# Expert weights as consecutive rows per partition, and a float32r scatter, in a two-layer transformer kernel

## The chip, the cores and the metric

The kernel runs on one core of a Trainium2 chip. The metric is the device time of one execution in microseconds (us); the time of a kernel is the median of several runs. Engines: PE is TensorE (matmul; PEld is its weight load), DVE is VectorE, ACT is ScalarE, POOL is GpSimd, and SP is the queue from which the DMAs here are issued. A product has a stationary operand, which is loaded into the array, and a moving operand, which streams through it; its result goes to one of eight PSUM banks.

## What is computed

Two transformer layers on 512 tokens of width 1024, all in float32. The change lies in the last part of the second layer: a mixture of experts in which each expert picks its tokens.

```python
def expert_choice_moe(h, w_router, w_gate, w_up, w_down):
    B, S, D = h.shape                                   # 1, 512, 1024
    cap = max(1, CAPACITY_FACTOR * S // N_EXPERTS)      # 64 tokens for each of 16 experts
    logits = jnp.einsum('bsd,de->bse', h, w_router).astype(jnp.float32)
    aff = jax.nn.softmax(logits, axis=-1)
    gate, idx = lax.top_k(aff.transpose(0, 2, 1), cap)
    xin = jax.vmap(lambda hb, ib: hb[ib])(h, idx)
    hid = jax.nn.silu(jnp.einsum('becd,edf->becf', xin, w_gate)) * jnp.einsum('becd,edf->becf', xin, w_up)
    y = jnp.einsum('becf,efd->becd', hid, w_down) * gate[..., None].astype(h.dtype)
    bidx = jnp.arange(B)[:, None, None]
    return jnp.zeros_like(h).at[bidx, idx].add(y)
```

h is the residual after an RMS norm with a gain, and the result is added to the residual. Each of the 16 experts has three matrices of 1024 x 1024, 4 MB each, so 201 MB in all are read from HBM.

## The kernel before

The program is recorded and not issued at once. A list scheduler with estimated lengths of the instructions puts all of them in an order for each engine, the longest remaining path first, and then issues them; each engine works through its own list strictly. Every instruction is issued in `emit`, so in the trace all carry the line L500, and they are told apart by engine, operation and shape.

The experts are worked through in eight **pairs**; the two experts of a pair use the lower and the upper 64 columns of the array side by side. The residual is `x2`, token-major: 128 tokens on the partitions, four token blocks `tb`, 1024 columns.

- `moe_begin` lists the weights in the order of their use, `ring` gives them eight slots of 2 MB, `load` and `load_to` issue the DMAs on SP as slots come free. A slot holds a half of a matrix: all 1024 rows and 512 columns, with row `128 k + p` on partition p. `pieces` cuts a half into DMAs of mostly 1 MB, four row blocks k each; a run in HBM is 512 columns, 2 KB. The last two halves come as column quarters, so that little work follows the last bytes.
- `ranks(p)` finds for each token its place among those that a pair's two experts could take. PE spreads each affinity over a row (128 x 128 products), VectorE compares (the arrays `ahead`) and counts, PE adds up the counts (128 x 1 products in bfloat16), VectorE puts the place together (`pos`).
- `gather(p)` makes two matrices of 512 tokens x 128 places. `O` has the norm's factor r2 of a token at its place, else zero, and `Og` has the token's affinity, its gate. PE gathers the pair's tokens by products whose stationary operand is 128 neighbouring columns of `x2` and whose moving operand is `O`; the result, already transposed, is scaled by the norm's gain into `XT`. `Og` is transposed into `OGT`.
- `prod(x)` multiplies gathered tokens with the next half of a matrix for both experts: 8 row blocks k, each a float32 product for either expert, 64 places x 512 columns.
- The loop at the end of `moe` makes, for each half h of the hidden columns, gate and up products, `s` = silu(g) * u, and transposes `s` by 128-column blocks into `HT`. Then for each half of the output columns it makes `y`, copies it to `ys`, and scatters: for each token block one float32 product of `OGT` with `ys`, added by VectorE to `acc`. The next pair's `gather` is called between up products and transposes.

## Time and profile before

| | |
|---|---|
| median of 3 runs (lowest to highest) | 3010.46 us (3009.56 to 3010.53) |
| span of the profiled execution, first to last instruction | 3006.1 us |
| PE busy in the span | 2937.9 us, 98% |
| VectorE busy | 1689.4 us, 56% |
| ScalarE busy | 655.6 us, 22% |
| expert loop in the span | 2502.6 to 3006.1, 503.5 us |

The span is the profiled execution's own time; around it lies what the device does before the first and after the last instruction. Busy shares average over stages that are unlike. In the first 2500 us the DMA engines moved around 100 GB/s, in the expert loop 363, so that loop is read on its own below. A group's busy time counts overlapping instructions once; float32 products show as two records each.

### The profile page before, as it was taken

To read this page: it belongs to the slowest core of one execution; us is meant where nothing else is said; L and a number is where in the kernel's file an instruction comes from. 1 tells how busy PE (TensorE), PEld (TensorE's weight loads), DVE (VectorE), ACT (ScalarE), POOL (GpSimd) and SP (SyncE) were. 2 spreads that over 40 slices of the span, in tenths; PEclk is the share of its full clock that TensorE was granted. 3 is DMA by queue.
4 is the path that set the end of the run, shared out by engine and by line. 5 is a ranking of instruction groups with operands and counts; after the bars stand their busy time and mean duration, and the time that the engine had idled before them with its cause. 6 is when DMAs were issued, how large, how long until landed. Compare 5 with 4: busy or idle time off the path is not lost.

```text
span 3006.1 us, 40850 instructions
## 1 busy us (share of the span) xinstructions
PE 2937.9 (98%) x16433; PEld 2274.2 (76%) x16433; DVE 1689.4 (56%) x3270; ACT 655.6 (22%) x1429; POOL 268.9 (9%) x275
## 2 busy tenths in 40 slices
PE   8999999999999999999999999999989999999999
PEld 7888898777888888888987778888778995444443
DVE  6555566776555555555668765555786763223221
ACT  3000124562000110001336620011232541000000
POOL 1000012111000000001121110000231210000000
PEclk9999999999999999999999999999999999999999
DMA  4333322102333333334221033333212367999997
GB/s 122 99 98 98 107 77 56 46 5 82 97 99 95 101 94 96 96 100 113 72 55 39 7 93 98 99 98 98 64 57 86 127 231 259 381 386 386 386 386 282
DMA packets 341091, 403.84 MB, mean 134 GB/s; under 512 B 37209, under 2 KB 242054, under 8 KB 340902
## 3 DMA queue, kind: packets, MB, share of 16 engines
q1 hardware_dynamic: 340742, 401.09, 41.0%
q8 instruction: 129, 2.11, 0.3%
q14 instruction: 60, 0.49, 0.1%
q0 software_dynamic: 160, 0.14, 0.0%
HBM read 399.09 MB, written 2.10 MB: 133 GB/s over the span
## 4 chain that ended last, share of the span: by engine, by line
PE 90%; DVE 6%; ACT 1%; issue 1%; DMA 1%; POOL 0%; SPq 0%; DVEq 0%; ACTq 0%
PE bank L500 90%; DVE arena L500 6%; ACT arena L500 1%; DMA arena<-in_mla_w_ukv 0%; DMA arena<-in_ffn_wg 0%; DMA arena<-in_ffn_wd 0%; POOL arena L500 0%; SPq L500 0%; DVEq L500 0%; ACTq L500 0%
## 5 line engine op out<-in xcount | busy, mean ns | idle before, releaser
L500 PE MATMUL bank<-arena 128*128 128x512 f32 (+9 forms) x16433 | 2937.9, 365 | 64.5 <-DVE arena L500 39.9
L500 PEld LDWEIGHTS bank<-arena 128*128 128x128 f32 (+3 forms) x16065 | 2261.3, 177 | 687.3 <-issue 274.4
L500 DVE TENSOR_TENSOR arena<-arena 128x1024 fp32r<-128x1024 f32 (+10 forms) x906 | 701.5, 791 | 38.7 <-PE bank L500 11.3
L500 DVE CAST arena<-arena 128x1024 fp32r<-128x1024 f32 (+5 forms) x392 | 252.4, 645 | 594.6 <-PE bank L500 423.3
L500 ACT ACTIVATE arena<-arena 128x512 f32<-128x512 f32 (+8 forms) x339 | 199.2, 614 | 857.6 <-DVE arena L500 787.2
L500 POOL TENSOR_TENSOR arena<-arena 128x512 f32<-128x512 f32 (+12 forms) x155 | 193.9, 1260 | 1847.0 <-ACT arena L500 796.3
L500 DVE TENSOR_TENSOR arena<-arena,bank 128x512 f32<-128x512 f32 (+2 forms) x265 | 160.4, 626 | 328.5 <-PE bank L500 327.7
L500 ACT COPY arena<-bank 128x512 f32<-128x512 f32 (+5 forms) x222 | 120.6, 552 | 532.5 <-PE bank L500 529.2
L500 ACT ACTIVATE arena<-bank,arena 128x256 f32<-128x256 f32 (+4 forms) x336 | 162.7, 509 | 236.8 <-DVE arena L500 128.0
L500 ACT CAST arena<-arena 128x512 fp32r<-128x512 f32 (+5 forms) x96 | 77.8, 816 | 503.1 <-DVE arena L500 423.9
L500 DVE TENSOR_TENSOR arena<-bank,arena 128x512 f32<-128x512 f32 (+3 forms) x207 | 134.7, 676 | 67.6 <-PE bank L500 49.2
L500 DVE TENSOR_REDUCE arena<-bank 128x1 f32<-128x512 f32 (+3 forms) x208 | 97.5, 481 | 22.4 <-PE bank L500 20.6
L500 DVE TENSOR_SCALAR arena<-bank,arena 128x128 f32<-128x128 f32 (+4 forms) x100 | 35.6, 395 | 126.2 <-PE bank L500 126.0
L500 DVE TENSOR_SCALAR arena<-arena 128x512 f32<-128x512 f32 (+12 forms) x305 | 95.0, 344 | 12.7 <-ACT arena L500 8.0
L500 DVE SCALAR_TENSOR_TENSOR arena<-arena 128x512 fp32r<-128x512 f32 (+8 forms) x162 | 88.2, 551 | 8.1 <-DMA arena<-in_attn_k_norm_w 4.2
L500 POOL TENSOR_SCALAR arena<-arena 128x512 f32<-128x512 f32 (+3 forms) x93 | 64.8, 698 | 239.9 <-DVE arena L500 207.1
L500 ACT CAST arena<-bank 96x512 fp32r<-96x512 f32 (+3 forms) x97 | 54.3, 580 | 70.2 <-PE bank L500 61.2
L500 PEld LDWEIGHTS <-arena 128*128 128x128 bf16 x368 | 27.4, 97 | 40.5 <-issue 17.9
L500 DVE SCALAR_TENSOR_TENSOR arena<-bank,arena 128x128 bf16<-128x128 f32 (+4 forms) x94 | 40.0, 449 | 31.5 <-PE bank L500 28.8
L500 DVE COPY arena<-bank 128x512 f32<-128x512 f32 (+9 forms) x63 | 34.3, 545 | 34.1 <-PE bank L500 33.1
L500 ACT ACTIVATION_READ_ACCUMULATOR arena<-bank,arena 128x1 f32 x208 | 42.5, 204 | 0.0
L500 ACT ACTIVATE arena<-bank 128x512 f32<-128x512 f32 (+2 forms) x28 | 16.5, 590 | 105.7 <-PE bank L500 86.0
(28 smaller groups left out, 201.3 us busy)
## 6 DMA issues: line engine op xcount, KB each, us to landing
arena<-in_w_expert_gate SPq DMA_DIRECT2D x56, 1024.0 KB
arena<-in_w_expert_up SPq DMA_DIRECT2D x56, 1024.0 KB
arena<-in_w_expert_down SPq DMA_DIRECT2D x48, 1024.0 KB
arena<-in_ffn_wg SPq DMA_DIRECT2D x88, 512.0 KB
arena<-in_ffn_wu SPq DMA_DIRECT2D x88, 512.0 KB
arena<-in_ffn_wd SPq DMA_DIRECT2D x80, 512.0 KB
arena<-in_w_in SPq DMA_DIRECT2D x68, 256.0 KB
arena<-in_w_in SPq DMA_DIRECT2D x32, 512.0 KB
```

What stands on the lines that cost most here:

```text
L500: last[i] = getattr(getattr(self.real, eng), m)(*a, **k).ins
```

## The change

A slot of the ring now holds a half of a matrix by **rows**: partition p has rows 8p to 8p + 3 or 8p + 4 to 8p + 7, all 1024 columns. A DMA of 1 MB takes two neighbouring rows for each partition, a run of 8 KB. The last two loads come in column pieces of 512, 256 and 256.

The contraction then runs over row `8 p + k` on partition p, so the other operands are taken with a step of eight: `x2[:, tb, k::8]` in the gather, `s[:, k::8]` in the transposes, and the gain in that layout, `g8`, by a small DMA of its own.

`prod` works on both column halves at once (two PSUM banks of the tag "a", of which there are four for three), one row half after the other. `s` is whole, 1024 wide, and the next pair's `gather` is called after all up products.

`O` is one exact one-hot matrix, made by one comparison. The norm's factor and the gate are gathered with it: four products of `O` with `fac` (two gates and two copies of r2 per pair) give `GR`, the gate and the factor of each place. The factor enters in silu's scale and in the up product, the gate in `y`. `Og` is gone.

The scatter uses the transposed one-hot `OT` in float32r and splits gated `y` in a rounded part `yh` and the rest `yl`: two float32r products for each token block, added up in PSUM, in place of one float32 product.

```diff
     def moe_begin(self, es):
-        wg, wu, wd = (self.a[f"w_expert_{n}_2"][0] for n in ("gate", "up", "down"))
         self.order = []
         for p in range(self.NE // 2):
-            for h in range(2):
-                for w in (wg, wu):
-                    self.order += [(2 * p + e, w, h) for e in range(2)]
-            for h in range(2):
-                self.order += [(2 * p + e, wd, h) for e in range(2)]
+            for n in ("gate", "up", "down"):
+                w = self.a[f"w_expert_{n}_2"][0]
+                self.order += [(2 * p + e, w, h) for h in range(2) for e in range(2)]
...
-            self.slots.append(p.tile([128, KC, 512], F32, name="ring"))
+            self.slots.append(p.tile([128, KC // 2, D], F32, name="ring"))
...
     def load_to(self, loads):
-        for c, k, m in self.pieces(loads[0][1]) if loads else ():
+        for k, m, c0, c1 in self.pieces(loads[0][1]) if loads else ():
             for t, n in loads:
                 e, w, h = self.order[n]
-                src = w[e].rearrange("(k p) c -> p k c", p=128)[:, k:k + m, 512 * h:512 * h + 512]
                 if n > 70:
                     self.nc.fifo.append(len(self.nc.ops))
-                if c is None:
-                    self.nc.sync.dma_start(t[:, k:k + m], src)
+                if c1 - c0 == D:
+                    src = w[e].rearrange("(p k) c -> p (k c)", k=KC)[:, (4 * h + k) * D:(4 * h + k + m) * D]
+                    self.nc.sync.dma_start(t.rearrange("p k c -> p (k c)")[:, k * D:(k + m) * D], src)
                 else:
-                    self.nc.sync.dma_start(self.split(t)[:, c, k:k + m], src[:, :, 256 * c:256 * c + 256])
+                    src = w[e].rearrange("(p k) c -> p k c", k=KC)[:, 4 * h + k:4 * h + k + m, c0:c1]
+                    self.nc.sync.dma_start(t[:, k:k + m, c0:c1], src)
+    LAST = ((0, 512), (512, 768), (768, 1024))
     def pieces(self, n):
-        m = 4 if 12 <= n < len(self.order) - 4 else 2
         if n < len(self.order) - 2:
-            return [(None, k, m) for k in range(0, KC, m)]
-        return [(c, k, 4) for c in range(2) for k in (0, 4)]
-    def split(self, t):
-        return t.rearrange("p k c -> p (k c)").rearrange("p (h k c) -> p h k c", h=2, k=KC)
+            return [(k, 2, 0, D) for k in (0, 2)]
+        return [(0, 4, c0, c1) for c0, c1 in self.LAST]
...
+        self.g8 = rp.tile([128, KC], F32, name="g8")
+        nc.sync.dma_start(self.g8, self.a["norm2_w_2"][0].rearrange("(p k) -> p k", k=KC))
...
+        fac = rp.tile([128, 4, NE // 2, 4], F32, name="fac")
         nc.vector.tensor_mul(aff, aff, bc(m4))
+        nc.vector.tensor_copy(fac[:, :, :, :2], aff.rearrange("p t (a b) -> p t a b", b=2))
+        nc.vector.tensor_copy(fac[:, :, :, 2:], r2[:, :, None, None].to_broadcast([128, 4, NE // 2, 2]))
...
-            cs = pp.tile([128, 2, 4], F32, name="a", bufs=3)
+            cs = pp.tile([128, 2, 4], F32, name="b", bufs=4)
...
-        XT, OGT = {}, {}
-        g2 = self.gain["norm2_w_2", 0]
+        XT, OT, GR = {}, {}, {}
         def gather(p):
-            O, Og = (mp.tile([128, 4, 2, CAP], F32, name=n, bufs=1) for n in ("O", "Og"))
-            es_ = slice(2 * p, 2 * p + 2)
+            O = mp.tile([128, 4, 2, CAP], F32, name="O", bufs=1)
             pos = ranks(p).rearrange("p e t -> p t e")
-            for tb in range(4):
-                for e in range(2):
-                    nc.vector.tensor_scalar(O[:, tb, e], self.iota, pos[:, tb, e:e + 1], r2[:, tb:tb + 1],
-                                            op0=ALU.is_equal, op1=ALU.mult)
-            nc.vector.tensor_tensor(Og, self.iota[:, None, None, :].to_broadcast([128, 4, 2, CAP]),
+            nc.vector.tensor_tensor(O, self.iota[:, None, None, :].to_broadcast([128, 4, 2, CAP]),
                                     pos[:, :, :, None].to_broadcast([128, 4, 2, CAP]), ALU.is_equal)
-            self.tt("tensor_mul", Og, Og, aff[:, :, es_, None].to_broadcast([128, 4, 2, CAP]))
+            O = [O[:, tb].rearrange("p a b -> p (a b)") for tb in range(4)]
             XT[p] = xp.tile([128, KC, 2 * CAP], F32, name="XT", bufs=2)
             for k0 in range(0, KC, 4):
                 ps = pp.tile([128, 4, 128], F32, name="b", tag="b", bufs=4)
                 for tb in range(4):
                     for d in range(4):
-                        nc.tensor.matmul(ps[:, d, :], x2[:, tb, 128 * (k0 + d):128 * (k0 + d) + 128],
-                                         O[:, tb].rearrange("p a b -> p (a b)"), start=tb + d == 0, stop=tb == 3,
+                        nc.tensor.matmul(ps[:, d, :], x2[:, tb, k0 + d::KC], O[tb], start=tb + d == 0, stop=tb == 3,
                                          skip_group_check=True)
                 for d in range(4):
-                    self.scaled(XT[p][:, k0 + d, :], ps[:, d, :], g2[:, k0 + d:k0 + d + 1])
+                    self.scaled(XT[p][:, k0 + d, :], ps[:, d, :], self.g8[:, k0 + d:k0 + d + 1])
+            ps = pp.tile([128, 4], F32, name="b", bufs=4)
+            for tb in range(4):
+                nc.tensor.matmul(ps, O[tb], fac[:, tb, p], start=tb == 0, stop=tb == 3)
+            GR[p] = mp.tile([128, 2], F32, name="gr", bufs=2)
+            for e in range(2):
+                rows = slice(64 * e, 64 * e + 64)
+                nc.vector.tensor_copy(GR[p][rows], ps[rows, e:3:2 - e])
             ps = pp.tile([128, T], F32, name="b", bufs=4)
             for tb in range(4):
-                nc.tensor.transpose(ps[:, 128 * tb:128 * tb + 128], Og[:, tb].rearrange("p a b -> p (a b)"), self.ident)
-            OGT[p] = mp.tile([128, T], F32, name="OGT", bufs=2)
-            self.copy(OGT[p], ps)
+                nc.tensor.transpose(ps[:, 128 * tb:128 * tb + 128], O[tb], self.ident)
+            OT[p] = mp.tile([128, T], F32R, name="OT", bufs=2)
+            self.copy(OT[p], ps)
         it = [0]
-        def prod(x, c=None):
-            n = 512 if c is None else 256
-            ps = pp.tile([128, n], F32, name="a", bufs=3)
-            ws = [self.slot(it[0] + e) for e in range(2)]
...
-            if c != 0:
+        def prod(x, cols=((0, 512), (512, 1024))):
+            ps = [pp.tile([128, c1 - c0], F32, name="a", tag="a", bufs=4) for c0, c1 in cols]
+            for h in range(2):
+                ws = [self.slot(it[0] + e) for e in range(2)]
+                split = [[c] for c in range(len(cols))] if h and len(cols) > 2 else [range(len(cols))]
+                for cs in split:
+                    for k in range(4):
+                        for c in cs:
+                            with nc.atomic():
+                                for e in range(2):
+                                    nc.tensor.matmul(ps[c][64 * e:64 * e + 64], x[:, 4 * h + k, 64 * e:64 * e + 64],
+                                                     ws[e][:, k, cols[c][0]:cols[c][1]], start=h + k == 0,
+                                                     stop=h == 1 and k == 3, skip_group_check=True)
                 it[0] += 2
                 if it[0] != 4:
                     self.load(2)
...
         outv = self.out
         last = self.NE // 2 - 1
         for p in range(last + 1):
+            gate, r = GR[p][:, 0:1], GR[p][:, 1:2]
+            g = prod(XT[p])
+            if p == 0:
+                e_early.close()
+                ap, hp = pool("moe_acc"), pool("moe_h", "right")
+                acc = ap.tile([128, 4, D], F32, name="acc")
+            s = hp.tile([128, D], F32, name="hs")
+            for c in range(2):
+                nc.scalar.activation(s[:, 512 * c:512 * c + 512], g[c], AF.Silu, scale=r)
+            u = prod(XT[p])
+            for c in range(2):
+                x = s[:, 512 * c:512 * c + 512]
+                nc.vector.scalar_tensor_tensor(x, u[c], r, x, op0=ALU.mult, op1=ALU.mult)
+            if p < last:
+                gather(p + 1)
+            HT = hp.tile([128, KC, 2 * CAP], F32, name="HT")
             for h in range(2):
-                g = prod(XT[p])
-                s = mp.tile([128, 512], F32, name="hs")
-                nc.scalar.activation(s, g, AF.Silu)
-                u = prod(XT[p])
-                nc.vector.tensor_mul(s, s, u)
...
-                if h == 1 and p < last:
-                    gather(p + 1)
                 ps = pp.tile([128, 4, 128], F32, name="b", tag="b", bufs=4)
-                for f in range(4):
-                    nc.tensor.transpose(ps[:, f, :], s[:, 128 * f:128 * f + 128], self.ident)
+                for k in range(4):
+                    nc.tensor.transpose(ps[:, k, :], s[:, 4 * h + k::KC], self.ident)
                 self.copy(HT[:, 4 * h:4 * h + 4, :], ps)
-            for h in range(2):
-                for c in (None,) if p < last or h == 0 else (0, 1):
-                    y = prod(HT, c)
-                    n = 512 if c is None else 256
-                    ys = hp.tile([128, 512], F32, name="ys", bufs=2)[:, :n]
-                    self.copy(ys, y)
-                    for tb in range(4):
-                        ps = pp.tile([128, n], F32, name="b", bufs=4)
-                        nc.tensor.matmul(ps, OGT[p][:, 128 * tb:128 * tb + 128], ys, start=True, stop=True)
-                        at = slice(512 * h + 256 * (c or 0), 512 * h + 256 * (c or 0) + n)
-                        nc.vector.tensor_add(acc[:, tb, at], acc[:, tb, at] if p else x2[:, tb, at], ps)
-                        if p == last:
-                            nc.sync.dma_start(outv[128 * tb:128 * tb + 128, at], acc[:, tb, at])
+            cols = self.LAST if p == last else ((0, 512), (512, 1024))
+            for y, (c0, c1) in zip(prod(HT, cols), cols):
+                n = c1 - c0
+                yh, yl = (hp.tile([128, 512], F32R, name=m, bufs=2)[:, :n] for m in ("yh", "yl"))
+                self.scaled(yh, y, gate)
+                nc.vector.scalar_tensor_tensor(yl, y, gate, f32(yh), op0=ALU.mult, op1=ALU.subtract)
+                for tb in range(4):
+                    ps = pp.tile([128, n], F32, name="b", bufs=4)
+                    o = OT[p][:, 128 * tb:128 * tb + 128]
+                    nc.tensor.matmul(ps, o, yh, start=True, stop=False)
+                    nc.tensor.matmul(ps, o, yl, start=False, stop=True)
+                    nc.vector.tensor_add(acc[:, tb, c0:c1], acc[:, tb, c0:c1] if p else x2[:, tb, c0:c1], ps)
+                    if p == last:
+                        nc.sync.dma_start(outv[128 * tb:128 * tb + 128, c0:c1], acc[:, tb, c0:c1])
```

How the instructions stand on the engines, at the seam between the second and the third pair (the second of seven). On PE, where the scatter ends and the ranks begin; 128x512 rows are the scatter, 128x128 rows the spreading of affinities, 128x1 rows the counts, 64x512 rows expert products. Before:

```order
L500 MATMUL bank_62<-arena 128x512
L500 MATMUL bank_61<-arena 128x512
L500 MATMUL bank_63<-arena 128x128
L500 MATMUL bank_59<-arena 128x128 x4
L500 MATMUL bank_63<-arena 128x128 x3
L500 MATMUL bank_61<-arena 128x128 x4
L500 LDWEIGHTS arena
L500 MATMUL bank_62<-arena 128x1
L500 LDWEIGHTS arena
L500 MATMUL bank_62<-arena 128x1
L500 MATMUL bank_63<-arena 64x512 x2
```

and in the changed kernel:

```order
L500 MATMUL bank_63<-arena 128x512
L500 MATMUL bank_59<-arena 128x512 x2
L500 MATMUL bank_62<-arena 128x512 x2
L500 MATMUL bank_65<-arena 128x512 x2
L500 MATMUL bank_64<-arena 128x128 x4
L500 MATMUL bank_63<-arena 128x128 x4
L500 LDWEIGHTS arena
L500 MATMUL bank_62<-arena 128x1
L500 LDWEIGHTS arena
```

The scatter has two products for each bank, and no expert products stand between the counts.

On PE at the same seam, from the last count over the gather (the 32 products of 128x128) and the transposes of the one-hot matrix and of s, to the next expert products. Before:

```order
L500 MATMUL bank_62<-arena 128x1
L500 MATMUL bank_65<-arena 64x512 x4
L500 MATMUL bank_62<-arena 128x128 x9
L500 MATMUL bank_65<-arena 64x512 x4
L500 MATMUL bank_62<-arena 128x128 x7
L500 MATMUL bank_61<-arena 128x128 x8
L500 MATMUL bank_62<-arena 64x512 x8
L500 MATMUL bank_61<-arena 128x128 x8
L500 MATMUL bank_59<-arena 128x128
L500 MATMUL bank_64<-arena 128x128 x4
```

and in the changed kernel:

```order
L500 MATMUL bank_62<-arena 128x1
L500 MATMUL bank_62<-arena 128x128 x16
L500 MATMUL bank_65<-arena 128x128 x16
L500 MATMUL bank_62<-arena 128x4 x4
L500 MATMUL bank_63<-arena 128x128
L500 MATMUL bank_64<-arena 128x128 x4
L500 MATMUL bank_62<-arena 128x128 x4
L500 MATMUL bank_63<-arena 128x128 x3
L500 MATMUL bank_64<-arena 64x512 x2
```

The gather is one run, with the four GR products (128x4) after it; the expert products that stood around and inside it stand behind the transposes.

On VectorE at the same seam, from the end of the ranks: the place of each token, the matrices for gather and scatter, and what comes next. Before:

```order
L500 TENSOR_REDUCE arena<-arena 128x8
L500 TENSOR_TENSOR arena<-arena 128x8
L500 TENSOR_TENSOR arena<-arena,bank_65 128x8
L500 TENSOR_SCALAR arena<-arena 128x64 x8
L500 TENSOR_SCALAR arena<-bank_65,arena 128x128 x3
L500 TENSOR_SCALAR arena<-bank_61,arena 128x128 x4
L500 TENSOR_TENSOR arena<-arena 128x512 x2
```

and in the changed kernel:

```order
L500 TENSOR_TENSOR arena<-arena,bank_65 128x512
L500 TENSOR_REDUCE arena<-arena 128x8
L500 TENSOR_TENSOR arena<-arena 128x8
L500 TENSOR_TENSOR arena<-arena,bank_62 128x8
L500 TENSOR_TENSOR arena<-arena 128x512
L500 TENSOR_SCALAR arena<-bank_62,arena 128x128 x3
L500 TENSOR_SCALAR arena<-bank_65,arena 128x128 x3
L500 COPY arena<-bank_62 64x2 x2
```

One comparison makes O in place of eight, the product with the gates is gone, and one scatter addition still stands ahead of the place.

## Rows read from the trace of the kernel before

**Rows 1.** expert stage, five stretches: busy us (instructions) by engine, clock, DMA share, GB/s

```profile
2502.60:3006.10 503.50, 492.81 (x2517) 210.67 (x2516) 128.35 (x421) 36.47 (x68) 0.00 (x0) 1.00 0.99 363
2622.50:2683.60 61.10, 61.10 (x324) 27.44 (x322) 17.05 (x58) 4.29 (x8) 0.00 (x0) 1.00 1.05 386
2745.70:2809.20 63.50, 63.15 (x324) 26.95 (x322) 16.36 (x55) 5.75 (x12) 0.00 (x0) 1.00 1.05 386
2809.20:2878.70 69.50, 68.44 (x330) 27.53 (x326) 19.46 (x61) 4.98 (x9) 0.00 (x0) 1.00 1.05 387
2878.70:2943.50 64.80, 62.85 (x321) 26.50 (x320) 17.32 (x58) 4.39 (x8) 0.00 (x0) 1.00 1.04 386
2943.50:3006.10 62.60, 56.59 (x265) 21.27 (x264) 10.93 (x19) 3.69 (x7) 0.00 (x0) 1.00 0.74 261
```

**Rows 2.** PE timeline in the stage: start, us, first instruction, count [idle before]

```profile
2561.24 180.64 PE L500 MATMUL bank<-arena 128*64 128x512 f32 x944 [0.35 <-ACT arena L500]
2742.23 59.67 PE L500 MATMUL bank<-arena 128*64 128x512 f32 x304 [0.35 <-ACT arena L500]
```

**Rows 3.** DMA queue, 2580 to 2960 us: packets, MB, share of 16 engines

```profile
DMA packets 73801, 146.79 MB, mean 386 GB/s; under 512 B 2252, under 2 KB 2252, under 8 KB 73780
q1 hardware_dynamic: 73780, 146.50, 104.3%
```

**Rows 4.** waits in the stage: us in total, times, longest us

```profile
PEld bank L500 <- DMA arena<-in_w_expert_gate: 1.3, 3, 0.8
PEld bank L500 <- DMA arena<-in_w_expert_down: 1.1, 3, 0.8
PEld bank L500 <- DMA arena<-in_w_expert_up: 0.6, 2, 0.3
```

**Rows 5.** by form: MLP, compression, HGRN (two), product, gather, its loads, scatter

```profile
L500 PE MATMUL bank<-arena 128*128 128x512 f32 x443 | 100.6, 389 | 0.0
L500 PE MATMUL bank<-arena 128*64 128x62 f32 x64 | 3.7, 287 | 0.0
L500 PE MATMUL bank<-arena 128*128 128x128 f32 x9 | 1.6, 329 | 0.0
L500 PE MATMUL bank<-arena 128*128 128x128 f32 x8 | 1.6, 344 | 0.6 <-DVE arena L500 0.6
L500 PE MATMUL bank<-arena 128*64 128x512 f32 x64 | 14.0, 594 | 0.3 <-ACT arena L500 0.3
L500 PE MATMUL bank<-arena 128*128 128x128 f32 x20 | 2.4, 275 | 0.0
L500 PEld LDWEIGHTS bank<-arena 128*128 128x128 f32 x19 | 2.2, 192 | 0.0
L500 PE MATMUL bank<-arena 128*128 128x512 f32 x11 | 4.9, 592 | 0.0
```

**Rows 6.** groups by form in the stage: count, busy us, mean ns, idle

```profile
L500 PE MATMUL bank<-arena 128*128 128x1 bf16 x140 | 8.5, 166 | 0.0
L500 PE MATMUL bank<-arena 128*128 128x256 f32 x16 | 4.0, 392 | 0.0
```

**Rows 7.** timeline of VectorE at one seam (pair 2 to 3)

```profile
2658.26 0.35 DVE L500 SCALAR_TENSOR_TENSOR arena<-bank,arena 128x128 bf16<-128x128 f32 x1 [0.31 <-PE bank L500]
...
2662.86 0.69 DVE L500 TENSOR_TENSOR arena<-arena,bank 128x512 f32<-128x512 f32 x1
2663.47 0.17 DVE L500 TENSOR_REDUCE arena<-arena 128x8 f32<-128x16 f32 x1
...
2664.13 1.88 DVE L500 TENSOR_SCALAR arena<-arena 128x64 f32<-128x64 f32 x8
2665.92 1.41 DVE L500 TENSOR_TENSOR arena<-arena 128x512 f32<-128x512 f32 x2
```

**Rows 8.** groups by form on PE: scatter in the sixth stretch

```profile
L500 PE MATMUL bank<-arena 128*128 128x512 f32 x24 | 12.2, 623 | 0.7 <-ACT arena L500 0.7
```

**Rows 9.** strip loads, 2394 to 2397 us, in 40 bins: GB/s

```profile
GB/s 55 137 164 246 410 410 382 355 246 273 410 410 355 437 437 437 355 410 246 164 28 27 27 0 0 0 0 0 0 0 0 48 191 143 143 96 96 0 96 48
```

More of the change, by code (lines that the diff above doesn't have):

```diff
@@ L1826, in ring @@
             p = self.es_ring.enter_context(self.nc.tile_pool("ring", side=side))
-            self.slots.append(p.tile([128, KC, 512], F32, name="ring"))
+            self.slots.append(p.tile([128, KC // 2, D], F32, name="ring"))
             self.load()
     def early(self, es, side):
-        t = es.enter_context(self.nc.tile_pool("early", side=side)).tile([128, KC, 512], F32, name="early")
+        t = es.enter_context(self.nc.tile_pool("early", side=side)).tile([128, KC // 2, D], F32, name="early")
         self.first.append(t)
@@ L1992, in gather @@
-            OGT[p] = mp.tile([128, T], F32, name="OGT", bufs=2)
-            self.copy(OGT[p], ps)
+                nc.tensor.transpose(ps[:, 128 * tb:128 * tb + 128], O[tb], self.ident)
+            OT[p] = mp.tile([128, T], F32R, name="OT", bufs=2)
+            self.copy(OT[p], ps)
         it = [0]
-        def prod(x, c=None):
-            n = 512 if c is None else 256
-            ps = pp.tile([128, n], F32, name="a", bufs=3)
-            ws = [self.slot(it[0] + e) for e in range(2)]
-            if c is not None:
-                ws = [self.split(u)[:, c] for u in ws]
-            for k in range(KC):
-                with nc.atomic():
-                    for e in range(2):
-                        nc.tensor.matmul(ps[64 * e:64 * e + 64], x[:, k, 64 * e:64 * e + 64], ws[e][:, k],
-                                         start=k == 0, stop=k == KC - 1, skip_group_check=True)
-            if c != 0:
+        def prod(x, cols=((0, 512), (512, 1024))):
[11 more added lines that the diff above has]
+                                                     stop=h == 1 and k == 3, skip_group_check=True)
@@ L2018, in moe @@
         for p in range(last + 1):
-            for h in range(2):
-                g = prod(XT[p])
-                s = mp.tile([128, 512], F32, name="hs")
-                nc.scalar.activation(s, g, AF.Silu)
-                u = prod(XT[p])
-                nc.vector.tensor_mul(s, s, u)
-                if p + h == 0:
-                    e_early.close()
-                    ap, hp = pool("moe_acc"), pool("moe_h", "right")
-                    acc = ap.tile([128, 4, D], F32, name="acc")
-                if h == 0:
-                    HT = hp.tile([128, KC, 2 * CAP], F32, name="HT", bufs=2)
-                if h == 1 and p < last:
-                    gather(p + 1)
+            gate, r = GR[p][:, 0:1], GR[p][:, 1:2]
```

## Prediction

> **What bounds the kernel now.** The stage that the diff touches is the expert loop. The table by stretches gives it 503.5 of the span's 3006.1 us, at a granted clock of 1.00 throughout, so no term below needs a clock; PE is busy for 492.81 of them [rows 1]. The timeline of PE shows that this busy time is all but unbroken: 180.64 us without a gap, later pieces parted by some tenths [rows 2]. Then I asked what else is full. From 2580 to 2960 us the DMA queue moved 386 GB/s, its engines' share at 104% [rows 3]. So two resources run at their limit side by side. Which one ends last is in the table of waits: PE's weight loads waited 1.3 + 1.1 + 0.6 = 3.0 us in all for expert weights [rows 4]. PE bounds the stage, and the transfers follow closely. VectorE is busy for 128.35 us, a quarter [rows 1]: what it does costs nothing as long as products stand in PE's queue meanwhile. So I price the change on PE, ask whether PE still has those products, then whether the DMAs could take over.
>
> **How I read a pace.** Instructions overlap in the records, so a group's busy time less one mean, over the count less one, is the time from start to start. A float32 product appears as two records (passes), a float32r product or a transpose as one. From [rows 5]: the float32 scatter pass, 128 x 512, (4.9 - 0.592) / 10 = 0.431 us; the float32r pass of that shape (the first block's MLP) (100.6 - 0.389) / 442 = 0.227; the float32 pass of 128 x 128 (2.4 - 0.275) / 19 = 0.112; an expert pass of 64 x 512 (14.0 - 0.594) / 63 = 0.213, one in each half of the columns side by side. The expert products keep their number and shapes, so they cost the same after.
>
> **1. Scatter.** 120 passes at 0.431 become 120 float32r passes at 0.227 (for yh and yl): 120 x 0.204 = 24.5 us less. The last pair's 16 passes of half the width [rows 6] go from half of 0.431 to half of 0.227: 1.6 less. Together **-26.0**, all on PE, which is the path.
>
> **2. GR.** Four new float32 products of 128 x 4 in each of 8 gathers, two passes each, with a stationary of 128 columns: 64 passes. The nearest rows are the 128 x 1 bfloat16 pass, 8.5 / 140 = 0.061 us [rows 6], and the 128 x 128 pass, 0.112. Its stationary being float32, I take the upper: 64 x 0.112 = **+7.2** (3.9 to 7.2).
>
> **3. The stride of eight.** To match weights stored as eight consecutive rows per partition, x2 and s are read with a step of 8 columns, as the stationary operand. Per pair that is 32 gather products of two passes and 8 transposes of one; over 8 pairs 512 + 64 = 576 passes. No stationary operand of before has a step, so this is bounded. Below: zero, if loading a stepped stationary is as fast or hides behind the pass before it. Near: the HGRN stage has 128 x 128 float32 passes whose moving operand jumps between two rows at each element; they take (1.6 - 0.329) / 8 = 0.159 and (1.6 - 0.344) / 7 = 0.179 us against 0.112 [rows 5], so 0.047 to 0.067 more. Above: the compression of the NSA mixer reads 62 columns with a step of 16, two products side by side, in (3.7 - 0.287) / 63 x 2 = 0.108 us, that is 1.75 ns a column; 128 columns would take 0.224, or 0.112 more. I take the HGRN rows, whose shape is the gather's own, at 0.055: 576 x 0.055 = **+31.7** (0 to 64.5). One row speaks against the zero: at the 0.112 pace the weight loads fill all the time too (19 loads busy for 2.2 us in a stretch of 1.95, [rows 5]), so a longer load has nothing to hide behind.
>
> **4. The seams.** Between two pairs VectorE finds the ranks and builds O, and only then may PE gather. Before, the ranks took it from 2658.26 to 2662.86, 4.6 us, then came an addition of 0.69, three small steps (0.17 the first, 0.5 together), eight comparisons of 1.88 and two matrices of 1.41 [rows 7]. PE hardly waited: its scatter passes of 0.431, two for each token block, let VectorE's additions keep up, and its queue holds expert products between the 128 x 1 rows and after them. In the new order the scatter's products, the ranks' and the gather's follow one another at seams 1 and 2 with no expert product between. Seam 2: after the last product of u, VectorE has two products of s and eight additions at 0.69 (6.9), the ranks (4.6), the small steps (0.5) and O (0.69), with some 0.3 to hand over: 13.0. PE has 13 scatter passes (3.0), 16 of the ranks (1.8) and 20 of 128 x 1 (1.2): 6.0. It waits about 7. Seam 1 has no additions yet: 7.5 against 3.0, some 4.5. At seam 3 eight expert products (16 passes, 3.4 us) stand between: VectorE's additions, ranks, small steps and O, 12.2 with what precedes them, against 16 scatter passes (3.6), 3.0 and 3.4: it waits 2. Later seams have sixteen, and this short sum ends there: 14. Walking both queues row by row, with the places of the additions in VectorE's order, I found 3.6, 7.9, 5.4, 2.9, 2.1, 1.5 and 1.5 = 24.9. I take **+20**, between the two; ends 8 (half of the short sum, were the other half covered) and 27. Behind the wait stand, on PE, the gather, HT's transposes and the next y; ScalarE and SP wait with it. SP's loads wait for ring slots that PE frees, but eight slots of 2 MB are 43 us at 386 GB/s, so a wait of 8 starves nothing.
>
> **5. Late pairs.** Stretches 5 to 7 took 63.5, 69.5 and 64.8 us against 61.1 in the third [rows 1]. The sixth holds 24 scatter records [rows 8], eight more than a pair has, 3.4 us at 0.431. Left are 2.4 + 5.0 + 3.7 = 11.1 us, of which 3.0 are named as waits for weights [rows 4]. A later PE, and shorter transfers, take those away. I take twice what is named, about half of the whole, **-6** (0 to -11).
>
> **6. The last pair** has no gather to hide behind: two products of s and two copies of HT stand open before y, 2.8 with each at VectorE's 0.69: **+2.5** (0 to 2.8).
>
> At nothing: yl on VectorE, the two small copies of GR, fac and the small load of g8, hidden by PE's products outside the seams; SP's loads keep their size and number. If the cover of yl went, it would cost 16 x 0.69 = 11.
>
> **The DMAs.** A run is 8 KB where it was 2 KB. Loads with runs of 3.5 KB reach 410 to 437 GB/s in their fullest bins [rows 9], against 386 for the expert weights [rows 3]. At 421, the 146.5 MB of those 380 us would take 348, so the weights land some 32 us earlier. That buys nothing where PE is last, but it decides what a faster PE could gain.
>
> The Trainium skill (DMA: Bandwidth & Descriptors, Where 436 GB/s comes from) speaks against such a gain: for transfers from HBM to SBUF the HBM side, about 358 GB/s, binds. The trace's 386 is above that figure, so as a number it doesn't hold here; by the rule the loads would stay where they are, and the sum with them, since PE is last in it.
>
> **The sum.** -26.0 + 7.2 + 31.7 + 20 - 6 + 2.5 = +29.4 us on a span of 3006.1: 3035.5. The median, 3010.46, is 4.4 above that span, and I carry this over: **3040 us**, 1% slower.
>
> **Rivals.**
> A, *the stride is free* (0.30). For it: a load can run under the pass before. Against it: loads of that shape already fill the time of the passes. The sum without term 3 is -2.3: 3008. The seams decide the sign: with under 16 us of waits it is faster by over 0.2%, with 8 it comes to 2996. The Trainium skill (TensorE: Matmul & The Clock Gate, the table at its head) says that PE's queue pulls weight loads ahead of matmuls in flight; that is this rival's mechanism, and no row here shows it for a stepped operand.
> C, *the stride costs what the 62-column row says* (0.12): 64.5 for 31.7, 3073.
> D, *the loads don't get faster and PE does* (0.08), so the change doesn't do what it says. The last stretch moved 261 GB/s for 62.6 us, 16.3 MB, of which 2.1 are the output [rows 1]: at 386 the weights have landed 37 us into it, near 2980, and some 26 us of work follow. A faster PE then runs into the transfers, and the end stays near 3006 of span, 3010. Rows 9 speak against it.
>
> **How the numbers follow.** Forecast 0.50, with 3020 to 3058 for itself (seams 8 to 27, stride 0.047 to 0.067, late pairs 0 to -11). About 0.2%, 6 us, is what a measurement of this kernel can tell from no change. Faster: 0.19 of A, 0.03 of D, 0.01 of the forecast, together 0.23. Same: 0.08 of A, 0.05 of D, 0.03 of the forecast, 0.16. Slower: the other 0.61. The range leaves out C (0.12) and the lowest of A (some 0.05): 2996 to 3062.
>
> **What would show it.** Scatter passes from 0.431 to 0.227 in the groups by form; gather passes at 0.16 to 0.18 from start to start (0.112 for A, 0.22 for C); PE's timeline with a hole before each gather, largest at seam 2, released by VectorE; DMA bins above 400 GB/s, then pauses, since PE is last. I'm wrong if the gathers pace at 0.112, if the holes are missing because the queues fall otherwise than I walked them, or if the expert products slow down beside the longer runs, which no row of before can tell.

## The result, and the profile after

The changed kernel takes **3057.98 us** (median of 4 runs, 3054.24 to 3059.16) against 3010.49 us for the kernel before: a ratio of 1.0155, 95% interval 1.0142 to 1.0167. It is slower by 47.5 us, as forecast in sign, inside the range of 2996 to 3062, and 18 us above the forecast of 3040. The profiled execution has a span of 3057.4 us, 51.3 more than that of before.

Up to 2491 us the two traces run side by side (PE's records of equal number start within 0.6 us of each other). All of the difference lies in the expert stage. Three of its groups before, by form (count | busy us, mean ns | idle before):

```profile
L500 PE MATMUL bank<-arena 128*128 128x128 f32 x727 | 93.9, 284 | 2.0 <-DVE arena L500 2.0
L500 PE MATMUL bank<-arena 128*128 128x512 f32 x120 | 58.2, 614 | 1.4 <-ACT arena L500 1.4
L500 PEld LDWEIGHTS bank<-arena 128*128 128x128 f32 x861 | 108.7, 189 | 73.2 <-issue 58.6 <-DVE arena L500 8.6 <-ACT arena L500 5.6
```

and its groups on PE with their weight loads after:

```profile
L500 PE MATMUL bank<-arena 128*64 128x512 f32 x1504 | 332.8, 597 | 1.2 <-ACT arena L500 1.1
L500 PEld LDWEIGHTS bank<-arena 128*128 128x128 f32 x928 | 179.9, 271 | 34.2 <-issue 17.0 <-DVE arena L500 11.5 <-ACT arena L500 1.2
L500 PE MATMUL bank<-arena 128*128 128x128 f32 x729 | 156.0, 377 | 6.5 <-DVE arena L500 6.5
L500 PE MATMUL bank<-arena 128*128 128x512 f32 x120 | 33.0, 413 | 0.0
L500 PE MATMUL bank<-arena 128*128 128x1 bf16 x160 | 13.2, 169 | 9.6 <-DVE arena L500 7.6
L500 PE MATMUL bank<-arena 128*128 128x4 f32 x64 | 7.6, 242 | 0.0
```

The scatter did what it should: 33.0 us for 120 passes, where it was 58.2. The 128 x 128 group is the one that stands out, 156.0 us for 93.9, and the loads of its stationary operands with it. One gather by itself, the third pair's, is 32 products of two passes each:

```profile
L500 PE MATMUL bank<-arena 128*128 128x128 f32 x64 | 15.5, 419 | 1.7 <-DVE arena L500 1.7
```

From start to start that is (15.5 - 0.419) / 63 = 0.239 us a pass. The gather of before ran at 0.112 ([rows 5], the row of 20 passes). The transposes of `s` have the same step of 8 and don't show this price. The last pair, which has no gather, has its eight in one piece:

```profile
L500 PE MATMUL bank<-arena 128*128 128x128 f32 x8 | 1.2, 288 | 0.9 <-DVE arena L500 0.9
```

The median from start to start there is 0.112 us; in the variant without a step (step1, below) it is 0.110.

Idle time hides inside "busy" where records overlap. So I added up, for each form, the time from each PE record's start to the next one's start, from 2490 us to the last. A wait counts here for the record that stands before it. Microseconds, with four of the experiments below:

| form | before | after | step1 | after_seam | step1_seam | f32r_only |
|---|---|---|---|---|---|---|
| 128x128 (ranks, gather, transposes) | 92.6 | 154.1 | 99.0 | 150.4 | 95.7 | 92.9 |
| 128x1 (counts; the wait for O follows the last) | 11.0 | 26.3 | 35.2 | 10.6 | 15.2 | 15.6 |
| 64x512 (expert products) | 341.1 | 331.9 | 329.5 | 334.5 | 333.5 | 347.8 |
| 128x512 (scatter) | 56.1 | 31.8 | 30.9 | 31.5 | 31.8 | 32.9 |
| 128x4 or 128x2 (GR, gates) | - | 6.5 | 6.8 | 6.6 | 6.9 | 6.1 |
| last pair's narrow ones | 11.6 | 10.4 | 10.4 | 10.4 | 14.5 | 10.7 |
| sum | 512.4 | 561.0 | 511.8 | 544.0 | 497.6 | 506.0 |

The DMA queue got its longer runs, and rests between them. GB/s in 40 bins and the totals from 2580 to 2960 us, after:

```profile
GB/s 419 418 419 422 417 128 124 424 418 423 416 421 417 11 388 420 418 421 417 422 168 240 425 420 418 420 422 310 162 423 419 420 422 416 387 106 425 419 420 417
DMA packets 19066, 138.90 MB, mean 366 GB/s; under 512 B 2125, under 2 KB 2125, under 8 KB 2125
```

421 where [rows 3] have 386, with a pause about once a pair: the queue waits for PE to free a slot of the ring. The waits of the stage (us in total, times, longest) say the same; PE waits for VectorE, hardly for weights:

```profile
PE bank L500 <- DVE arena L500: 13.2, 21, 1.7
PEld bank L500 <- DMA arena<-in_w_expert_up: 1.4, 5, 0.3
PEld bank L500 <- DMA arena<-in_w_expert_down: 0.7, 2, 0.4
```

### The profile page after: what moved, and what is told of

Same layout as the page of the kernel before. It is cut to its first block, busy times and chain, and to the rows that moved or that the text cites. A ratio compares the mean times of both kernels' runs of the same rounds, so it can differ in the third digit from the quotient of the medians.

```text
span 3057.4 us, 40897 instructions
## 1 busy us (share of the span) xinstructions
PE 2978.7 (97%) x16497; PEld 2350.6 (77%) x16497; DVE 1684.0 (55%) x3236; ACT 657.2 (21%) x1426; POOL 269.5 (9%) x275
## 4 chain that ended last, share of the span: by engine, by line
PE 89%; DVE 8%; DMA 1%; issue 1%; ACT 1%; POOL 0%; SPq 0%; DVEq 0%; ACTq 0%
PE bank L500 89%; DVE arena L500 8%; ACT arena L500 1%; DMA arena<-in_w_expert_gate 1%; DMA arena<-in_ffn_wd 0%; DMA arena<-in_x 0%; DMA arena<-in_mla_w_ukv 0%; DMA arena<-in_mla_w_uq 0%; POOL arena L500 0%; SPq L500 0%; DVEq L500 0%; DVEq L2148 0%; ACTq L500 0%
## 5 line engine op out<-in xcount | busy, mean ns | idle before, releaser
L500 PE MATMUL bank<-arena 128*128 128x512 f32 (+8 forms) x16497 | 2978.7, 367 | 72.5 <-DVE arena L500 48.8
L500 PEld LDWEIGHTS bank<-arena 128*128 128x128 f32 (+3 forms) x16129 | 2336.7, 182 | 662.0 <-issue 252.4
L500 ACT ACTIVATE arena<-bank,arena 128x256 f32<-128x256 f32 (+6 forms) x373 | 186.8, 522 | 640.8 <-PE bank L500 327.7
L500 DVE TENSOR_TENSOR arena<-arena,bank 128x512 f32<-128x512 f32 (+3 forms) x249 | 144.9, 620 | 153.3 <-PE bank L500 152.1
L500 DVE SCALAR_TENSOR_TENSOR arena<-bank,arena 128x128 bf16<-128x128 f32 (+5 forms) x127 | 64.9, 523 | 217.4 <-ACT arena L500 153.2
L500 ACT COPY arena<-bank 128x512 f32<-128x512 f32 (+5 forms) x198 | 107.3, 550 | 252.7 <-PE bank L500 248.8
L500 DVE TENSOR_SCALAR arena<-arena 128x512 f32<-128x512 f32 (+14 forms) x241 | 80.0, 353 | 12.7 <-ACT arena L500 8.3
L500 DVE COPY arena<-bank 128x512 f32<-128x512 f32 (+8 forms) x78 | 36.2, 464 | 31.2 <-PE bank L500 30.2
L500 DVE RECIPROCAL arena<-arena 128x1 f32<-128x1 f32 (+2 forms) x249 | 36.7, 161 | 4.9 <-ACT arena L500 4.5
```

Source lines behind the costliest of these rows:

```text
L500: last[i] = getattr(getattr(self.real, eng), m)(*a, **k).ins
```

## The experiments

**What does a step cost?** In the kernel before, the gather of pair p reads x2 with a step of p + 1 columns (other columns than the reference's).

```diff
+        def col(k, p):
+            n = 127 * (p + 1) + 1
+            at = min(128 * k, D - n)
+            return slice(at, at + n, p + 1)
...
-                        nc.tensor.matmul(ps[:, d, :], x2[:, tb, 128 * (k0 + d):128 * (k0 + d) + 128],
+                        nc.tensor.matmul(ps[:, d, :], x2[:, tb, col(k0 + d, p)],
```

> The kernel before, with one edit: the gather of pair p (0 to 7) reads x2 with a step of p + 1 columns, so that each pair gathers other columns than the reference's; the number and shapes of all instructions stay. It measures the price of the step alone, without longer DMA runs and without the new seams. Theory (a stepped stationary operand is slower to load, by the 16-byte lines that it touches, as the changed kernel's 0.238 us per pass of 128 columns suggests): passes of the gather at 0.112 us from start to start for steps 1 and 2, between for 3, and 0.238 for 4 to 8. Rival 1 (the price grows with the step): 0.112 to 0.238 in even parts, about 0.018 per step, with 0.13 at step 2. Rival 2 (the gather of the changed kernel is slow for another reason, the denser DMA writes into SBUF or waits within the run): 0.112 at every step.

One run measured all eight steps. PE by form, one stretch inside each gather, steps 1 to 8 in order:

```profile
L500 PE MATMUL bank<-arena 128*128 128x128 f32 x26 | 3.1, 275 | 0.0
L500 PE MATMUL bank<-arena 128*128 128x128 f32 x29 | 3.7, 285 | 0.0
L500 PE MATMUL bank<-arena 128*128 128x128 f32 x29 | 5.3, 341 | 0.0
L500 PE MATMUL bank<-arena 128*128 128x128 f32 x21 | 5.2, 402 | 0.0
L500 PE MATMUL bank<-arena 128*128 128x128 f32 x25 | 5.8, 387 | 0.0
L500 PE MATMUL bank<-arena 128*128 128x128 f32 x24 | 5.6, 390 | 0.0
L500 PE MATMUL bank<-arena 128*128 128x128 f32 x27 | 6.5, 398 | 0.0
L500 PE MATMUL bank<-arena 128*128 128x128 f32 x21 | 5.3, 408 | 0.0
```

From start to start, by the sum of above: 0.113, 0.122, 0.177, 0.240, 0.226, 0.227, 0.235, 0.245 us. (Each stretch holds a slower first pass or two; the medians are 0.112, 0.118, 0.173, 0.233, 0.220, 0.222, 0.230 and 0.240.) The theory holds: nearly free at a step of 2, half of the price at 3, all of it at 4, and no more beyond. A step of 1 to 4 floats touches a quarter, a half, three quarters and one 16-byte line for each column, and 0.24 times that is 0.06, 0.12, 0.18 and 0.24. So it reads as one line in 0.24 / 128 = 1.9 ns, an estimate. The first value lies below the 0.112 that a load takes without a step: the passes of GR, with four moving columns only, stand 0.112 us apart too (median in the changed kernel). The dip at steps of 5 to 7 is not explained by lines, and neither are the transposes of `s`, which a step of 8 leaves at 0.112; why they are spared stays open.

The first rival, an even growth with the step, falls: nothing is added after 4. The second, contention from the DMA writes or waits within the run, falls too: the loads here are those of the kernel before. This one execution took 3052.3 us, 41.9 more than the kernel before; the eight prices over 0.113, for 64 passes each, add up to 43.6.

The Trainium skill (SBUF — State Buffer, Door 1: The DMA port swizzle) names such 16-byte lines and puts the free stride at 4 fp32. The lines agree with the gather of these runs; the figure doesn't, since a step of 4 pays the whole price here (0.240 us) and one of 2 almost nothing (0.122).

**The same loads with a smaller step.** If two consecutive rows lie on a partition instead of eight, a run is still 8 KB (two rows of 4 KB), and the step is 2. With single rows, 128 k + p, a run is 4 KB and there is no step.

```diff
-                    src = w[e].rearrange("(p k) c -> p (k c)", k=KC)[:, (4 * h + k) * D:(4 * h + k + m) * D]
+                    src = w[e].rearrange("(q p j) c -> q p (j c)", p=128, j=2)[2 * h + k // 2]
...
-x2[:, tb, k0 + d::KC]
+x2[:, tb, 256 * ((k0 + d) // 2) + d % 2:256 * ((k0 + d) // 2) + 256:2]
```

> The changed kernel with two consecutive rows per partition in place of eight: row 256 q + 2 p + j lies on partition p, a run in HBM stays 8 KB, and x2 and s are read with a step of 2. Theory (the step by 16-byte lines): the gather's passes return to 0.112 us, the 576 stepped passes give back about 61 us, and the kernel takes 2997 us, faster than before by some 13. Rival 1 (a price in proportion to the step): 0.13 per pass, about 10 us more, 3007. Rival 2 (longer DMA runs or waits make the gather slow): no gain, 3058.

> The changed kernel with the weights' rows as before, row 128 k + p on partition p, but whole rows of 1024 columns: runs of 4 KB, no step in any operand. Theory: gather passes at 0.112 us, as in the variant with a step of 2; the loads run between 386 and 421 GB/s, about 405; 2997 us if PE is last, up to 3003 if the loads hold it. Rival (waits or contention make the gather slow): 3050 or more.

Measured 3014.26 us with a step of 2 (ratio to before 1.0013, 1.0004 to 1.0023) and 3011.32 us without one (1.0002, 0.9993 to 1.0011). The mechanism holds: the 128 x 128 forms fall from 154.1 to 107.8 and 99.0 us, with the longer runs in place. The sizes miss 2997 by 17 and 14 us. Without a step, the counts rose from 26.3 to 35.2 us, and the 128 x 128 forms gave back 55 us and not 61. The schedule came out another way, with no expert products left between the counts and the gather at five of the seams, where the changed kernel has three. One of the variant without a step looks like this (windows; busy us of PE, PEld, VectorE, ScalarE, POOL, then the granted clock, DMA share, GB/s):

```profile
2600.00:2604.00 4.00, 3.08 (x28) 2.41 (x26) 4.00 (x18) 0.00 (x0) 0.00 (x0) 1.00 1.03 410
2604.00:2609.00 5.00, 1.62 (x12) 1.21 (x13) 4.20 (x20) 0.00 (x0) 0.00 (x0) 0.64 1.03 410
2609.00:2612.00 3.00, 3.00 (x16) 3.00 (x15) 0.00 (x0) 0.00 (x0) 0.00 (x0) 0.50 1.02 408
2613.00:2615.00 2.00, 2.00 (x20) 2.00 (x19) 0.87 (x3) 0.00 (x0) 0.00 (x0) 1.00 1.01 401
```

PE stands for 4.3 of 9 us while VectorE works. The clock falls to 0.50, the 1.2 GHz level, and stays there as the gather starts: the passes of the gather stand 0.213 us apart there, then 0.112. So a seam costs its wait and then the first passes at half pace. That is the price that the expectation had left out.

**Filling the seams.** The banks of one tag are handed out in the order of the recording, and in the changed kernel the next pair's ranks, the gather and HT all stand in one row there, so HT's transposes, and with them the products of y, can't move ahead of the ranks. I recorded the ranks and O of pair p + 2 ahead of pair p's scatter, and raised their priority by 15 us:

```diff
+            if p + 2 <= last:
+                place(p + 2)
             cols = self.LAST if p == last else ((0, 512), (512, 1024))
...
+        def place(p):
+            nc.boost = 15000 if p else 0
             O = mp.tile([128, 4, 2, CAP], F32, name="O", bufs=1)
```

> The changed kernel (step of 8) with the seams filled in the same way, nothing else. Theory: the rows of 128 x 1 took 15 us more than before, so 3058 less 15 us, 3043; the stepped passes stay at 0.238 and keep it well behind the kernel before. Rival (the stride isn't the main cost, the seams are): 3020 or less.

> The variant without a step (rows 128 k + p, 4 KB runs), with the ranks and the one-hot matrix of pair p + 2 recorded ahead of pair p's scatter and given a priority 15 us higher in the schedule, so that expert products stand beside VectorE's work at the seams 2 to 7. Theory (the seams cost their waits and the passes at half the clock after them): in the variant without it the rows of 128 x 1 took 35.2 us from start to start against 11.0 in the kernel before, and some 47 more passes ran at 0.213; so 24 + 5 us less, of which seam 1 keeps 4: 2986 us. Rival 1 (the waits only move elsewhere, onto other products): 3005 to 3011. Rival 2 (the loads at 409 GB/s hold it): not under 2985, with waits for expert weights near the end.

> The variant with a step of 2 (8 KB runs), with the seams filled in the same way. Theory: 3014 less some 25 us, 2990; a little slower than the variant without a step, by the 9 us that its passes of 128 x 128 took more, unless the loads (421 against 409 GB/s) give that back. Rival (waits move elsewhere): 3010.

Measured: with the step of 8 **3044.67 us** (1.0117, 1.0102 to 1.0132); without a step **2992.64** (0.9944, 0.9929 to 0.9958); with a step of 2 **2991.05** (0.9942, 0.9927 to 0.9956), for an expected 2990. The first is 13 us under the changed kernel, for an expected 15, and its counts are back at 10.6 us. Its rival, that the seams are the main cost, falls: with the seams filled the step still keeps it 35 us behind the kernel before. In the variant with a step of 2, PE's timeline (start, us, first instruction, count, idle before) has holes at the first seam (the first rows here) and then one piece of 188.92 us, three pairs long:

```profile
2540.58 0.18 PE L504 MATMUL bank<-arena 128*128 128x1 bf16 x1 [0.36 <-DVE arena L504]
2541.26 1.00 PE L504 MATMUL bank<-arena 128*128 128x1 bf16 x8 [0.50 <-DVE arena L504]
2543.46 188.92 PE L504 MATMUL bank<-arena 128*128 128x128 f32 x1064 [1.21 <-DVE arena L504]
2732.59 28.93 PE L504 MATMUL bank<-arena 128*128 128x128 f32 x150 [0.20 <-DVE arena L504]
```

The variant without a step missed its 2986 by 7. It waited for the weights of its last product, as its second rival said: the rows below name these weights, where the variant with 8 KB runs has 0.3 us for them. From start to start the last pair's narrow products took 4.1 us more (14.5 in the table for 10.4), so this is some 4 of the 7. Waits in the stage, without a step:

```profile
PEld bank L504 <- DMA arena<-in_w_expert_down: 5.6, 5, 2.3
PE bank L504 <- DMA arena<-in_w_expert_down: 2.8, 3, 1.7
```

**Are the longer runs worth anything?** Both kinds of kernel, with the loads cut by columns to runs of 2 KB:

```diff
-            return [(k, 2, 0, D) for k in (0, 2)]
+            return [(0, 4, c, c + 512) for c in (0, 512)]
```

> The changed kernel with its loads cut by columns: the rows of a partition are the same (step of 8, seams as they are), but a run is 512 columns, 2 KB. Theory (PE is last in the changed kernel, the longer runs buy nothing there): 386 in place of 421 GB/s, hardly a pause of the queue, and 3055 to 3062 us. Rival (the long runs already pay in the changed kernel): 3070 or more, with PE's waits for weights.

> The variant without a step and with filled seams, its loads cut by columns: 512 of 1024, runs of 2 KB as in the kernel before, the same bytes per DMA. Theory (once PE is quick, the run length of the loads decides): 386 GB/s, the last weights land near 2980 us of the span, PE waits for weights 15 to 20 us in all, 3003 to 3008. Rival (PE is last all the same, longer runs buy nothing): within 3 us of the variant with 4 KB runs.

In the changed kernel: 3064.81 us (1.0183, 1.0168 to 1.0199), 7 us more and 3 above the upper end of what was expected. Waits for weights stayed at 2.7 us, so it isn't the loads that hold PE; PE's waits for VectorE rose from 13.2 to 20.9, and the order of PE differs a little with the pieces. From start to start the 7 us are spread over the 128 x 128 forms (3.0 more), the expert products (2.6) and the counts (2.5). Why the order came out so stays open. In the quick variant: **3018.7** (1.0032, 1.0021 to 1.0044) for 2992.64, 26 us. There the run length decides, and the time is 11 us over the expected upper end. The expert products take 357.8 us from start to start for 333.5. Queue from 2560 to 2960 us, and PE's waits:

```profile
DMA packets 77290, 153.79 MB, mean 384 GB/s; under 512 B 2332, under 2 KB 2332, under 8 KB 77268
```

```profile
PEld bank L504 <- DMA arena<-in_w_expert_down: 14.8, 11, 2.6
PEld bank L504 <- DMA arena<-in_w_expert_up: 14.0, 6, 3.7
PE bank L504 <- DMA arena<-in_w_expert_up: 9.3, 5, 2.8
PE bank L504 <- DMA arena<-in_w_expert_down: 7.5, 7, 1.7
```

Why later than the kernel before, at the same 386? From 2500 to 2560 us, before and this variant:

```profile
DMA packets 9483, 18.78 MB, mean 313 GB/s; under 512 B 336, under 2 KB 336, under 8 KB 9480
```

```profile
DMA packets 6340, 12.64 MB, mean 211 GB/s; under 512 B 192, under 2 KB 192, under 8 KB 6336
```

6.1 MB, at 386 GB/s 16 us, are missing at the start of the stream: in this variant the queue stands still from about 2544 us on and issues its next load at 2560.2, after a wait of 25 us for PE. The changed kernel moves as little there (12.62 MB), the float32r scatter in the old order 16.83. So the longer runs first seem to repay a loss that the new order of the halves makes; the old order with filled seams was not run.

**The float32r scatter alone**, in the kernel before: Og is a one-hot matrix, its gates are gathered, y is split; loads and order of the weights stay.

> The kernel before with the float32r scatter alone: Og is a one-hot matrix, the gate of each place comes from four small products of Og with the gates, and y is split in two float32r parts; loads, order of the weights and the gather's step are as before. PE has 120 x 0.2 + 1.5 = 26 us less in the scatter and 32 small products (64 passes, 7 us) more. Theory (two limits side by side: with loads at 386 GB/s the weights have all landed only near 2980 us of the span): 3006 to 3012, the gain shows up as PE's waits for weights. Rival (PE alone decides): 2991.

Measured **3002.63 us** (0.9973, 0.9963 to 0.9983), between the two. The scatter gave 23.2 us back (56.1 to 32.9); 6.1 went to the gates' products, 4.6 to the counts, 6.7 to expert products, about 4 of them in two waits for weights (at 2966 and 2979 us) and the rest in short waits for ScalarE and VectorE. The loads run at 386 without a pause, as theory said, and PE waits for the last ones. The bound was 3 to 9 us too high, because I kept 26 us of work behind the last weights; PE's last wait for them ended at 2980 us, and 20 us followed; the shorter scatter, 8 wide and 16 narrow passes, shortens that by some 3 too.

**A version that beats both.** The variant with a step of 2, its first seam filled as well (a second buffer for O, a higher priority for the first pair's one-hot transposes and the second pair's ranks):

> The variant with a step of 2 and filled seams, its first seam filled as well (a second buffer for the one-hot matrix, a higher priority for the first pair's last gather steps and for the second pair's ranks). Theory: the holes before the second gather (0.47 + 0.36 + 0.50 + 1.21 us) and the passes at half the clock behind them go, 2991 less some 4 us: 2987. Rival (the loads at 420 GB/s hold it): 2991.

**2989.28 us** (0.9930, 0.9914 to 0.9947): 0.7% faster than the kernel before, 2.2% faster than the changed one. Beside the 2991.05 of the one without that edit the gain lies within the intervals, so neither the theory's 2987 nor the rival's 2991 is shown. Only some of the holes before the second gather went: 2.5 us in four pieces became 1.86 in one.

## Why the prediction was right, and where its number was wrong

- **Bound on PE, transfers not last**: right. The waits for weights are 2.1 us after, and the queue pauses.
- **Step 1, scatter**, forecast -26.0: 24.3 in the wide passes and some 1 in the last pair's narrow ones, -25.5. The float32r pass took (33.0 - 0.413) / 119 = 0.27 with its stalls; the median from start to start is 0.23.
- **Step 2, GR**, +7.2: +6.5.
- **Step 3, the stride**, +31.7: **this is the term that failed**. The 128 x 128 forms rose by 61.5 us. The count of passes was wrong as well: the 64 transposes pay nothing, and the 512 gather passes pay 0.126 each (0.238 for 0.112), 64.5 us; the rest of the form took 3 less. I took the price from the HGRN rows, 0.159 to 0.179, because they have the gather's shape; but there it is the moving operand that jumps, between two rows, and here the stationary operand is loaded with the step. The row that I set as the far end, 62 columns with a step of 16, gave 0.224, near the 0.239 measured. That was rival C, to which I gave 0.12, and its number came out by luck: there too the operand with the step is the moving one (`kcT[..., ::16]`), and its two loads of 64 columns could set those 0.108 us just as well, since a load of 128 took 0.112 in GR's passes. No row of before had a stepped stationary operand; only a run like the ladder prices it.
- **Step 4, the seams**, +20 (8 to 27): +15.3 in the counts after; the holes are where they were forecast, the largest at seam 2, released by VectorE. The row by row walk's 24.9 was nearer to the variants without a step (24.2 more than before). The clock behind the holes was missing from the step. In the changed kernel it cost little, since the gather's stepped passes stand 0.238 us apart at either clock; windows of seam 2, after:

```profile
2615.80:2619.20 3.40, 1.03 (x9) 0.62 (x9) 3.20 (x17) 0.00 (x0) 0.00 (x0) 0.50 1.02 424
2619.20:2623.00 3.80, 3.77 (x16) 3.78 (x16) 0.00 (x0) 0.00 (x0) 0.00 (x0) 0.50 1.02 420
2627.00:2631.00 4.00, 4.00 (x19) 4.00 (x18) 0.87 (x3) 0.37 (x1) 0.00 (x0) 1.00 0.82 340
```

  The weight loads fill these windows too (3.78 of 3.8 us, and 4.00 of 4). What paid there is the work without that price: behind this gather, at 0.50 again, the transposes stood 0.213 us apart for 0.11.
- **Step 5, late pairs**, -6: the expert products took 9.2 us less, inside the 0 to -11, but not for the reason given. Waits for weights fell only from 3.0 to 2.1 us. Before, other work cuts the expert products into 84 pieces, after into 34, and some 9 of the 9.2 us lie in the first and last passes of these pieces.
- **Step 6, the last pair**, +2.5: not to be told apart; of the 51.3 us, the forms' sums leave 2.7 at the ends of the stage.

The forms sum to 48.6. Without step 3 the forecast summed to -2.3, the trace to -12.9; step 3 came out 30 us higher. So the other errors took 11 of its 30 us back. That the range held is partly luck: it left rival C out, and C's price, or nearly, is what the gather pays. Rival A fell with the ladder: from a step of 3 on, the load of a stepped stationary operand takes longer than the pass before it and doesn't hide behind it. The Trainium skill's rule that PE's queue pulls weight loads ahead (TensorE: Matmul & The Clock Gate, the table at its head) doesn't help there: weight loads already follow one another without a pause, 3.78 us of them in 3.8. Rival D fell too: the loads went from 386 to 421.

## What to carry to other kernels

When a layout is changed for longer DMA runs, look first at who then reads with a step. For the stationary operand of a float32 product, count the 16-byte lines per element: two consecutive float32 rows per partition gave the same 8 KB runs here, at a step that cost almost nothing. And price it by a row, or a run, with the step on the same operand. Two limits that run side by side have to be moved together: the scatter alone gave 8 us, and both together, with the step taken away and the seams filled, some 20. The longer runs alone, with the old scatter, were not run. And when work leaves an engine's queue, see what it was covering; a hole of a few microseconds on PE is paid twice, by the wait and by the passes at the lower clock behind it.

## What the runs showed of the hardware

- Gather passes of a float32 product, with a stationary operand of 128 columns, stand 0.11 us apart without a step, 0.12 with a step of 2, 0.18 with 3 and 0.22 to 0.25 with 4 to 8 (ladder). That fits one 16-byte line in about 1.9 ns, an estimate. At a step of 8 it is 0.238 at a granted clock of 0.50 and of 1.00 (changed kernel).
- Transposes with the same step of 8 stood 0.112 us apart (changed kernel), for 0.110 without a step (step1).
- Expert weights arrived at 386 GB/s in runs of 2 KB, 409 in 4 KB (step1) and 421 in 8 KB (changed kernel).
- After a seam with 4 us of holes in 9 the granted clock stood at 0.50 (1.2 GHz) for some 4 us more while PE was busy, and passes of 128 x 128 then stood 0.213 us apart for 0.112 (step1).
